# Mix stage of a two-block network: TensorE's order written out, with paired-half differential attention and retention interleaved with dense products

## Chip, cores and metric

One core of a Trainium2 chip (trn2) runs the whole network in one launch. The metric is the time of one execution on the device in microseconds (us). Of three runs shown the median was 3139.04 us, the lowest 3138.15 and the highest 3143.01.

## What is computed

All data are float32: 512 tokens (after the first block 528, with 16 learned tokens ahead of them) of 1024 features. A first block (attention of three kinds, then a wide feed-forward layer) is followed by two layers of a second block. Each of these two layers is a feed-forward layer, a *mix* stage and another feed-forward layer. The mix stage, with h the normalized input:

```
proj = h @ w_in                                   # 1024 -> 3584 columns
rq, rk, rv, rg, dq, dk, dv = split(proj)          # 512 columns each
# differential attention, 4 heads, each with two maps m of 64 features:
s[m] = q[m] @ k[m].T / 8        (causal);  p[m] = softmax(s[m])
o    = (p[0] - lam * p[1]) @ v;  o = rmsnorm(o) * subln_w * (1 - lambda_init)
# retention, 4 heads of 128 features (q, k rotated by position):
o    = ((q @ k.T / sqrt(128)) * decay(i - j)) @ v;  o = layernorm(o) * gn_w * silu(rg)
x    = x + concat(o_retention, o_diff) @ w_out
```

In the first layer all 528 rows are computed, in the second only the 512 that are returned (keys and values still have 528).

## The kernel before

Activations lie feature-major: 8 tiles of 128 features by 528 tokens. Every operand of a dense product is held as a high and a low part (`fp32r`), and a product is three passes: high by high, high by low, low by high. A *dense product* (`gemm`, line 163) makes one 128-row tile of the result: 8 slices of the 1024 features by 3 passes by 2 segments of 264 tokens, 48 matmuls into two PSUM tiles `ps_g` (line 172). Where 512 tokens are wanted it is 24 matmuls of 512 columns. Weights come in blocks of 256 columns (`wblock`, line 156): one 512 KB load each per 1024 elements on SP's queue, a copy to the high part on ScalarE (line 139) and a subtraction to the low part on VectorE (line 140).

`mix` (line 1217) runs through these steps: products for the values of differential attention (`v_heads`, `v_major`, transposed to token-major with the first 16 tokens in a fifth slot); twice: products for q and k of two heads, rotation (`rotate`, line 1378), split into halves (`stack`, line 1398), and `diff_heads` (line 1434) on the two heads; products for the values of retention; twice: products for q and k of two heads and `ret_head` (line 1510) for each; the norm of differential attention's output (lines 1272 to 1284); products for the gates with Silu (lines 1285 to 1292); the norm of retention's output (lines 1293 to 1306); the output products.

A block of differential attention (`diff_block`, line 1452) takes 128 queries (block 0: the 16 learned tokens; the second layer has no block 0) against all keys up to them: 16, 144, 272, 400 or 528 columns. For each of the two maps the scores are a 128-row matmul (line 1467: the stationary tile holds q's high half above its low half, the moving tile k's high half twice), a 64-row matmul with k's low half (line 1468) and the causal mask, added on the diagonal as a bf16 matmul with the identity (line 1470). The last block's 528 columns are cut into two spans of 264. Then come the maximum (1472), the exponential with its sum (1479), two reciprocals, a pass that scales the second map (1487), a pass that joins the maps (1490), transposes on TensorE (1497, and 1501 for the 16 first keys) with their copies (1498, 1502), and the product with V: 128-row matmuls for whole blocks of keys (1504) and one with 16 rows for the first keys (1505). Matmuls of float32 that is not split, such as 1504, 1505, 1525 and 1534, are two instructions each. `diff_heads` orders the three parts of consecutive blocks one behind the other.

Outside the mix stage the first block has an attention of blocks (line 546): four 64-row score matmuls a head, on rows 0 to 63 for one head of a pair and on rows 64 to 127 for the other (line 760).

What sets the order: the program gives instructions with their data; a scheduler lays them out per engine before the run, by priority and by when their operands should be there, so dense products may be put between the steps of attention wherever TensorE would wait. Each engine then runs its own list strictly in that order, and waits on semaphores.

## Time and profile before

| | |
|---|---|
| median of three runs | 3139.04 us |
| profiled execution | 3133.03 us, its span 3131.2 us |
| instructions | 54851 |
| TensorE matmuls busy | 3101.2 us |
| VectorE busy | 2250.4 us |
| ScalarE busy | 1534.7 us |
| mean granted TensorE clock | 0.996 |

The profiled execution is one of its own, near the runs shown. PE is TensorE's matmul side, PEld its weight loads, DVE VectorE, ACT ScalarE, POOL GpSimd, SP the engine whose queue issues most loads. A duration of a matmul runs from its start to a modelled end and overlaps its neighbours, so what TensorE pays for one is the distance to the next start. A form such as `64*128 64x264 f32` means 64 rows of the array, a stationary tile of 128 columns, 264 moving columns. Idle time before a group is given with what ended it.

### The profile page before, as it was taken

The page shows a single profiled execution, that of the slowest core. Times are in us where ns is not written, and L with a number is a line of the kernel's source. Part 1 is how long each engine was busy: PE and PEld are TensorE (multiplying, and loading weights), DVE is VectorE, ACT ScalarE, POOL GpSimd, SP SyncE. Part 2 cuts the span into 40 slices and gives each one's busy share as a digit, 9 for nine tenths or more (in the row PEclk, how much of TensorE's full clock was granted, in tenths as well). Part 3 has the DMA queues.
Part 4 walks back from the last instruction along what each step waited for, and adds up shares of the span by engine and source line. Part 5 has one row for each costly group of instructions (what it writes and reads, how often), then busy time and mean ns, then how long its engine had stood idle before and what let it go on. Part 6 is the DMA issues. An engine that isn't in the chain of part 4 may idle for free.

```text
span 3131.2 us, 54851 instructions
## 1 busy us (share of the span) xinstructions
PE 3101.2 (99%) x22264; PEld 2869.7 (92%) x22264; DVE 2250.4 (72%) x4225; ACT 1534.7 (49%) x2968; POOL 30.9 (1%) x64
## 2 busy tenths in 40 slices
PE   8999999999999999999999999999999999999998
PEld 6876798989898999999889999999999988899998
DVE  6256677977878887775866877768777586687775
ACT  5346556655555554444643544444444464354443
POOL 1000000000000000000000000000000000000000
PEclk9999999999999999999999999999999999999999
DMA  6121256323233422332112232322323311223232
GB/s 212 60 66 60 89 166 202 105 88 102 101 108 101 135 78 93 102 118 87 52 55 78 82 102 89 101 95 95 102 94 111 100 58 62 71 82 108 95 108 75
DMA packets 96958, 304.41 MB, mean 97 GB/s; under 512 B 12199, under 2 KB 20799, under 8 KB 96576
## 3 DMA queue, kind: packets, MB, share of 16 engines
q1 hardware_dynamic: 90384, 286.63, 27.8%
q0 software_dynamic: 2720, 7.78, 0.8%
q10 hardware_dynamic: 3600, 6.49, 0.7%
q8 instruction: 174, 2.85, 0.4%
q14 instruction: 80, 0.66, 0.1%
HBM read 290.34 MB, written 14.45 MB: 97 GB/s over the span
## 4 chain that ended last, share of the span: by engine, by line
PE 95%; DMA 2%; DVE 1%; ACT 1%; issue 0%; ACTq 0%; SPq 0%; DVEq 0%
PE ps_g L172 35%; PE ps_g L278 18%; PE ps_g L276 9%; PE ps_s L172 8%; PE ps_g L206 7%; PE ps_o L276 5%; PE ps_g L579 2%; PE ps_o L206 1%; DMA tmp_p<-gates 1%; PE ps_s L1468 1%; PE ps_s L513 1%; PE ps_o L535 1%; PE ps_s L1525 1%; PE ps_o L1504 1%; PE ps_o L1534 1%; PE ps_t L494 1%
## 5 line engine op out<-in xcount | busy, mean ns | idle before, releaser
L140 DVE TENSOR_TENSOR wqL<-wraw,wqH 128x512 fp32r<-128x512 f32 (+1 forms) x676 | 604.9, 910 | 278.2 <-ACT wqH L139 270.7
L139 ACT CAST wqH<-wraw 128x512 fp32r<-128x512 f32 (+1 forms) x676 | 527.1, 796 | 511.2 <-PE ps_g L172 282.5
L172 PE MATMUL ps_g<-yL,wqH 128*128 128x264 f32 (+2 forms) x1520 | 429.7, 320 | 0.4 <-DVE yL L414 0.4
L172 PE MATMUL ps_g<-yH,wqH 128*128 128x264 f32 (+2 forms) x1520 | 429.6, 321 | 0.0
L172 PE MATMUL ps_g<-yH,wqL 128*128 128x264 f32 (+2 forms) x1520 | 429.0, 321 | 0.3 <-DVE wqL L140 0.2
L278 PE MATMUL ps_g<-t,wqH 128*128 128x256 f32 (+1 forms) x1760 | 326.5, 283 | 0.0
L172 PEld LDWEIGHTS ps_g<-yL,wqH 128*128 128x128 f32 x1520 | 264.1, 189 | 23.7 <-issue 4.2
L172 PEld LDWEIGHTS ps_g<-yH,wqH 128*128 128x128 f32 x1520 | 262.6, 189 | 21.6 <-issue 3.1
L172 PEld LDWEIGHTS ps_g<-yH,wqL 128*128 128x128 f32 x1520 | 262.4, 189 | 21.0 <-issue 2.6
L278 PEld LDWEIGHTS ps_g<-t,wqH 128*128 128x128 f32 x1760 | 272.3, 188 | 1.8
L278 PE MATMUL ps_g<-t,wqL 128*128 128x256 f32 (+1 forms) x880 | 248.4, 282 | 0.0
L139 ACT CAST wqH<-ws 128x1024 fp32r<-128x1024 f32 x100 | 105.2, 1052 | 126.4 <-PE ps_o L276 33.6
L278 PEld LDWEIGHTS ps_g<-t,wqL 128*128 128x128 f32 x880 | 165.9, 189 | 0.0
L276 PE MATMUL ps_g<-t,wqH 128*128 128x264 f32 (+1 forms) x800 | 148.5, 283 | 0.0
L172 PE MATMUL ps_s<-hL,wqH 128*128 128x264 f32 (+1 forms) x544 | 141.2, 317 | 0.0
L172 PE MATMUL ps_g<-hL,wqH 128*128 128x264 f32 (+1 forms) x544 | 141.2, 317 | 0.0
L172 PE MATMUL ps_g<-hH,wqL 128*128 128x264 f32 (+1 forms) x544 | 141.1, 317 | 0.0
L172 PE MATMUL ps_s<-hH,wqL 128*128 128x264 f32 (+1 forms) x544 | 141.1, 317 | 0.0
L172 PE MATMUL ps_g<-hH,wqH 128*128 128x264 f32 (+1 forms) x544 | 141.0, 317 | 0.0
L172 PE MATMUL ps_s<-hH,wqH 128*128 128x264 f32 (+1 forms) x544 | 140.9, 316 | 0.0
L258 DVE TENSOR_TENSOR ws<-wraw 128x512 f32<-128x512 f32 x100 | 69.2, 692 | 86.1 <-DMA wraw<-in_ffn_w_gate 34.8
L140 DVE TENSOR_TENSOR wqL<-ws,wqH 128x1024 fp32r<-128x1024 f32 x100 | 122.4, 1224 | 6.3 <-ACT wqH L139 2.6
(445 smaller groups left out, 8234.8 us busy)
## 6 DMA issues: line engine op xcount, KB each, us to landing
wraw<-in_ffn_w_gate SPq DMA_DIRECT2D x88, 512.0 KB, 3.6
wraw<-in_ffn_w_up SPq DMA_DIRECT2D x88, 512.0 KB, 3.6
wraw<-in_ffn_w_down SPq DMA_DIRECT2D x88, 512.0 KB, 3.5
wraw<-in_w_in SPq DMA_DIRECT2D x86, 512.0 KB, 3.7
wraw<-in_w_up SPq DMA_DIRECT2D x64, 512.0 KB, 3.7
wraw<-in_w_down SPq DMA_DIRECT2D x32, 512.0 KB, 3.5
wraw<-in_w_gate SPq DMA_DIRECT2D x24, 512.0 KB, 4.1
tmp_p<-gates ACTq DMA_DIRECT2D x24, 256.0 KB, 3.3
```

What stands on the lines that cost most here:

```text
L139: self.nc.scalar.copy(out=H, in_=raw)
L140: self.nc.vector.tensor_sub(out=L, in0=raw, in1=H.bitcast(F32))
L172: self.nc.tensor.matmul(t[:, :m], lhsT=a, rhs=b[:, o:o + m], start=(k == 0 and i == 0), stop=(k == nk - 1 and i == 2))
L206: self.nc.tensor.matmul(q[:, :m], lhsT=a, rhs=b[:, o:o + m], start=(k == 0 and i == 0), stop=(k == nk - 1 and i == 2))
L258: nc.vector.tensor_add(out=S[:, :512], in0=A21, in1=A22)
L276: nc.tensor.matmul(ps, lhsT=a, rhs=b, start=first, stop=last)
L278: nc.tensor.matmul(ps, lhsT=a, rhs=b, start=False, stop=last, skip_group_check=True)
L494: nc.tensor.transpose(pt[:, s * P:(s + 1) * P], p[:, s * P:(s + 1) * P], self.ident)
L513: nc.tensor.matmul(ps[:, c], lhsT=q[:, i * P:(i + 1) * P], rhs=k[:, lo * P:(i + 1) * P], start=True, stop=True)
L535: nc.tensor.matmul(ops[obase:obase + 64, i * P:(i + 1) * P], lhsT=V(kb), rhs=pT[:, s0:s0 + P], start=(kb == lo), stop=(kb == i))
L579: nc.tensor.matmul(ps[:, :256], lhsT=a[:, ts], rhs=w, start=(k == 0 and i == 0), stop=(k == KD - 1 and i == 2))
L1468: nc.tensor.matmul(ps[:nq, :e - a], lhsT=qm[r], rhs=k[2][r, a:e], start=False, stop=not dg)
```

## The change

- Dense products become generators that yield after each of their eight slices; `drain` runs one to its end, `weave` runs a main generator and, between its steps, an even share of the steps of a side generator.
- In `mix` TensorE's instructions are kept in the order in which the program gives them (`manual_schedule`); other engines are laid out as before. The two pairs of heads of differential attention (three steps a block: scores; V product of the block before the last; transposes of the last) run against the products for retention's values and against the gates. Retention's first pair runs against q and k of its second pair, the second pair against the norm and the output products of differential attention, and the norm of retention's output against the rest of these.
- Scores: for each span and map three 64-row matmuls, high by high, low by high, high by low, the two maps alternating on rows 0 to 63 and 64 to 127; then the masks. The last block is cut into 512 columns (PSUM tiles `ps_s`) and the first 16 (PSUM tiles `ps_g`). `parts` replaces `stack`: q is scaled before the split, and q and k have one high and one low tile each.
- Softmax: the maxima come negated; the second map is scaled by lambda and the ratio of the sums in the pass that joins the maps; the output is scaled by the reciprocal when it leaves PSUM. The pass of line 1487 is gone.
- V product: the first 16 keys are transposed as 128 columns and multiplied as a 128-row matmul, with V's fifth slot filled with zeros by POOL (block 0 keeps 16 rows).
- Weight blocks are asked for one block ahead of use; the rotation tables have two buffers for three; retention's outputs share buffers with the values; differential attention's output goes into tiles of the stage's input; the loads of the last output weights are issued after the stage.

```diff
+def drain(steps):
+    while True:
+        try:
+            next(steps)
+        except StopIteration as e:
+            return e.value
+
+def weave(main, n, side, m):
+    done = 0
+    for i, _ in enumerate(main):
+        while done < (i + 1) * m // n:
+            next(side, None)
+            done += 1
...
-    def gemm(self, W, n, ys, R, seg_outer=False, tag="g"):
+    def gemm_steps(self, W, n, ys, R, seg_outer=False, tag="g"):
...
                         self.nc.tensor.matmul(t[:, :m], lhsT=a, rhs=b[:, o:o + m],
                                               start=(k == 0 and i == 0), stop=(k == nk - 1 and i == 2))
+                yield
         return ps
+    def gemm(self, *args, **kw):
+        return drain(self.gemm_steps(*args, **kw))
...
+            order = [2, 3, 6, 7, 4, 5, 12, 13, 8, 9, 10, 11]
+            def wi(i):
+                for j in order[:2] if i not in order else order[:order.index(i) + 2]:
+                    if j not in blocks:
+                        blocks[j] = self.wblock(A["w_in2"][l, j], KD, step=1024)
+                return blocks[i]
...
+            def gates():
+                for i in (12, 13):
+                    for n in range(2):
+                        g = self.tmp("sg", 4)
+                        self.evac_mul(g, (yield from self.gemm_steps(wi(i), n, ys, R)), rb)
+                        nc.scalar.activation(out=g[:, s], in_=g[:, s], func=AF.Silu)
+                        sg.append(g)
...
+            with self.tc.manual_schedule(engines={nc.tensor.engine}):
+                drain(values(0, NMETA, V))
+                rot = self.rot_tables("rope", rb)
+                drain(queries(2, "diff"))
+                side = values(6, 0, U)
+                weave(diff(0), 6 * nb, side, 32)
+                drain(side)
+                drain(queries(4, "diff"))
+                rot = self.rot_tables("ret", rb)
+                side = gates()
+                weave(diff(2), 6 * nb, side, 32)
+                drain(side)
+                drain(queries(8, "ret"))
+                main, side = retain(0), queries(10, "ret")
+                weave(main, 24, side, 32)
+                drain(side)
+                main, side = retain(2), chain(diff_out(), out_a())
+                weave(main, 24, side, 20)
+                weave(ret_out(), 4, side, 16)
+                drain(side)
+            W = self.last_w(A["w_out2b"][l])
...
-            t = self.qp.tile([P, TT], F32, name="rot", tag="rot", bufs=3)
+            t = self.qp.tile([P, TT], F32, name="rot", tag="rot", bufs=2)
...
-    def stack(self, t, R, key):
...
+    def parts(self, t, R, scale=None):
+        H, L = [self.tmp("qk2", 10, dt=F32R) for _ in range(2)]
+        self.split(t, H, L, R.off, R.n, scale)
+        return H, L
...
-        out = self.qp.tile([P, 5, P], F32, name="vh", tag="vh", bufs=6)
+        out = self.qp.tile([P, 5, P], F32, name="vh", tag="vh", bufs=8)
+        nc.gpsimd.memset(out[:, 4], 0.0)
...
                 step = self.diff_block(b, lam, *args)
                 next(step)
+                yield
+                if last:
+                    next(last, None)
+                yield
                 if todo:
                     next(todo)
-                if last:
-                    next(last, None)
+                yield
                 last, todo = todo, step
-        if last:
-            next(last, None)
+        next(last, None)
         next(todo)
         next(todo, None)
...
+        spans = [(0, nk)] if nk <= 512 else [(NMETA, nk), (0, NMETA)]
+        r = [slice(64 * m, 64 * m + 64) for m in range(2)]
+        qs = slice(q0, q0 + nq)
+        pst = []
+        for i, (a, e) in enumerate(spans):
+            ps = [self.psum("sg"[i])[:nq, :e - a] for _ in range(2)]
+            for j, (x, y) in enumerate(((0, 0), (1, 0), (0, 1))):
+                for m in range(2):
+                    nc.tensor.matmul(ps[m], lhsT=q[x][r[m], qs], rhs=k[y][r[m], a:e], start=(j == 0),
+                                     stop=(j == 2 and i == 1))
+            if i == 0:
+                for m in range(2):
+                    nc.tensor.matmul(ps[m][:, e - a - nq:], lhsT=self.identb[:nq, :nq], rhs=self.dm[:nq, :nq],
+                                     start=False, stop=True)
+            pst.append(ps)
...
+        nc.vector.reciprocal(out=sm[:nq, 8:10], in_=sm[:nq, 4:6])
+        nc.vector.scalar_tensor_tensor(out=sm[:nq, 10:11], in0=sm[:nq, 4:5], scalar=sm[:nq, 9:10], in1=lam[:nq],
+                                       op0=ALU.mult, op1=ALU.mult)
         a = Pm[0]
+        nc.vector.scalar_tensor_tensor(out=a[:nq, :nk], in0=Pm[1][:nq, :nk], scalar=sm[:nq, 10:11], in1=a[:nq, :nk],
+                                       op0=ALU.mult, op1=ALU.add)
         yield
...
         for j in range(b):
+            nc.tensor.matmul(ops[:nq, :P], lhsT=aT[:, j * P:(j + 1) * P], rhs=V[:, j], start=(j == 0), stop=False)
+        kk = 16 if b == 0 else P
+        nc.tensor.matmul(ops[:nq, :P], lhsT=aT[:kk, m], rhs=V[:kk, 4], start=(b == 0), stop=True)
+        nc.vector.tensor_scalar(out=o_sb[:nq, b], in0=ops[:nq, :P], scalar1=sm[:nq, 8:9], scalar2=None, op0=ALU.mult)
```

`ret_head` yields after each score span and each output block: 11 steps a head. `values` and `queries` make the products for V, or for q and k, of two blocks of weights; `diff_out`, `out_a` and `ret_out` hold the former lines 1272 to 1284, 1307 to 1310 and 1294 to 1306, the first and the last with a yield after each head.

## Rows read from the trace of the kernel before

**Rows 1.** The page, part 1: busy us and share of each engine

```profile
PE 3101.2 (99%) x22264; PEld 2869.7 (92%) x22264; DVE 2250.4 (72%) x4225; ACT 1534.7 (49%) x2968; POOL 30.9 (1%) x64
```

**Rows 2.** Busy time by windows, both mix stages (PEclk, DMA, GB/s last)

```profile
1440.00:1748.00 308.00, 306.77 (x2320) 280.27 (x2320) 203.99 (x555) 144.37 (x371) 0.00 (x0) 1.00 0.20 65
2472.00:2769.00 297.00, 296.90 (x1989) 259.34 (x1988) 195.58 (x495) 137.93 (x335) 0.00 (x0) 1.00 0.20 67
```

**Rows 3.** Waits of TensorE, first mix stage (total us, times, longest)

```profile
PE ps_s L1525 <- DVE rw L1526: 0.9, 1, 0.9
PE ps_s L1467 <- ACT tmp_P L1479: 0.3, 1, 0.3
```

**Rows 4.** Timeline of TensorE, 1512.9 to 1516.4 (start us, duration us)

```profile
1512.93 0.28 PE L1467 MATMUL ps_s<-tmp_qk,tmp_qk 128*128 128x264 f32 x1
1513.14 0.39 PE L1468 MATMUL ps_s<-tmp_qk,tmp_qk 64*128 64x264 f32 x1
1513.46 0.39 PE L172 MATMUL ps_g<-yH,wqL 128*128 128x264 f32 x1
1513.68 0.28 PE L172 MATMUL ps_g<-yH,wqH 128*128 128x264 f32 x1
...
1514.57 0.83 PE L1504 MATMUL ps_o<-vh,tmp_aT 128*128 128x128 f32 x6
1515.33 0.48 PE L1505 MATMUL ps_o<-vh,tmp_aT 16*128 16x128 f32 x2
1515.75 0.51 PE L172 MATMUL ps_g<-yL,wqH 128*128 128x264 f32 x2
1516.10 0.41 PE L172 MATMUL ps_g<-yH,wqL 128*128 128x264 f32 x2
1516.34 0.41 PE L172 MATMUL ps_g<-yH,wqH 128*128 128x264 f32 x2
```

**Rows 5.** Lines 1468 and 1505 in the whole kernel (duration ns min/median/max)

```profile
L1468 PE MATMUL ps_s<-tmp_qk,tmp_qk x88: 179/385/452, 1489.9 to 2612.4; 64*128 64x264 f32 x32, 64*128 64x144 f32 x16, 64*128 64x272 f32 x16, 64*128 64x400 f32 x16
...
L1505 PE MATMUL ps_o<-vh,tmp_aT x72: 267/274/372, 1503.9 to 2619.6; 16*128 16x128 f32 x64, 16*16 16x128 f32 x8
```

**Rows 6.** Busy time by windows, TensorE's instructions of line 546 alone

```profile
121.16:121.70 0.54, 0.54 (x4) 1.00 0.00 0
121.71:122.15 0.44, 0.44 (x10) 1.00 0.78 214
```

**Rows 7.** Groups of instructions, first mix stage: softmax (busy us, mean ns)

```profile
L1472 DVE TENSOR_REDUCE sm<-ps_s 128x1 f32<-128x400 f32 x8 | 4.6, 570 | 1.8 <-PE ps_s L1470 1.7
L1477 DVE TENSOR_SCALAR sm<-sm 128x1 f32<-128x1 f32 x32 | 4.5, 143 | 0.1
...
L1490 DVE SCALAR_TENSOR_TENSOR tmp_P<-tmp_P,sm 128x528 f32<-128x528 f32 x4 | 3.0, 757 | 0.0
...
L1479 ACT ACTIVATION_READ_ACCUMULATOR tmp_P<-ps_s,sm 128x1 f32 x40 | 7.7, 193 | 0.0
...
L1479 ACT ACTIVATE tmp_P<-ps_s,sm 128x400 f32<-128x400 f32 x8 | 4.7, 586 | 1.4 <-DVE sm L1485 1.4
...
L1479 ACT ACTIVATE tmp_P<-ps_s,sm 16x16 f32<-16x16 f32 x8 | 2.1, 264 | 1.4 <-DVE sm L1477 1.3
...
L1498 ACT COPY tmp_aT<-ps_t 128x512 f32<-128x512 f32 x4 | 2.3, 574 | 0.0
```

**Rows 8.** Timeline of ScalarE around the table load for Silu, layer 0

```profile
1678.59 0.27 ACT L1282 ACTIVATE tmp_qk<-ps_o,vecs 128x16 fp32r<-128x16 f32 x1 [0.32 <-PE ps_o L1335]
1678.88 1.28 ACT L1291 ACT_TABLE_LOAD   x1
1680.20 0.65 ACT L1291 ACTIVATE tmp_sg<-tmp_sg 128x528 f32<-128x528 f32 x1
```

**Rows 9.** Groups of instructions, first mix stage: retention's output on VectorE

```profile
L1299 DVE TENSOR_SCALAR ro<-ro,rst,sd 128x128 f32<-128x128 f32 x16 | 4.5, 332 | 0.0
...
L1538 DVE BATCH_NORM_STATS2 bst<-ro 16x6 f32<-16x128 f32 x4 | 1.1, 282 | 3.1 <-ACT ro L1536 3.1
```

More of the change, by code (lines that the diff above doesn't have):

```diff
@@ L2 @@
 from contextlib import ExitStack
+from itertools import chain
 import numpy as np
@@ L1228, in mix @@
             lam = self.lam(l)
[L1229 to L1240 removed]
+            order = [2, 3, 6, 7, 4, 5, 12, 13, 8, 9, 10, 11]
+            blocks = {i: w for i, w in enumerate(self.pre)}
+            def wi(i):
[3 more added lines that the diff above has]
+                return blocks[i]
+            V, U, sg = {}, {}, []
             od = [qp.tile([P, 5, P], F32, name="od", tag="od", bufs=4) for _ in range(4)]
@@ L1307, in mix, with values @@
-            for nb in range(4):
-                W = self.wblock(A["w_out2a"][l, nb], 4, step=1024)
-                for n in range(2):
-                    self.add_x(self.gemm(W, n, yd, R), 2 * nb + n)
+            nb = 5 if R.off == 0 else 4
+            def values(i0, c0, out):
+                late = None
+                for h in range(4):
+                    ps = yield from self.gemm_steps(wi(i0 + h // 2), h % 2, ys, R2, i0 == 0 and h == 0)
+                    if i0 == 0 and h == 0:
+                        self.late()
+                    if late:
+                        out[h - 1] = late()
+                    late = self.v_heads(ps, rb, c0)
+                self.vlate = lambda: out.update({3: late()})
@@ new lines, in queries @@
+            def queries(i0, use):
+                out = []
+                for j in range(2):
+                    for n in range(2):
+                        ps = yield from self.gemm_steps(wi(i0 + j), n, ys, (R, R2)[j] if use == "diff" else R2)
+                        if self.vlate:
+                            self.vlate()
+                            self.vlate = None
+                        if use == "diff":
+                            out.append(self.parts(self.rotate(ps, rot, True), (R, R2)[j], None if j else SCALE))
+                        else:
+                            out.append(self.rotate(ps, rot, False))
+                self.qk = out[:2], out[2:]
@@ new lines, in out_a, with ret_out @@
+            def out_a():
+                for b in range(4):
+                    W = self.wblock(A["w_out2a"][l, b], 4, step=1024)
+                    for n in range(2):
+                        self.add_x((yield from self.gemm_steps(W, n, yd, R)), 2 * b + n)
+            def ret_out():
+                rc = self.rsqrt_small(rst[:, :, :, 1], 1.0, 1.0)
+                for h in range(4):
+                    o, p = ro[h], sg[h]
+                    for b in range(5):
+                        nq = P if b < 4 else NMETA
+                        nc.vector.tensor_scalar(out=o[:nq, b], in0=o[:nq, b], scalar1=rst[:nq, h, b, 0:1],
+                                                scalar2=rc[:nq, h, b:b + 1], op0=ALU.subtract, op1=ALU.mult)
+                    for pt, c0, m in self.feature_major(o, 0, R):
+                        sl = slice(c0, c0 + m)
+                        nc.vector.scalar_tensor_tensor(out=p[:, sl], in0=pt, scalar=self.v(f"gn_w_{l}", h), in1=p[:, sl],
+                                                       op0=ALU.mult, op1=ALU.mult)
+                    yr.append(self.y_tile(4 + h))
+                    self.split(p, yr[h][0], yr[h][1], R.off, R.n)
+                    yield
@@ L1364, in lam @@
         nc.scalar.activation(out=e[:, :2], in_=ps[:, :2], func=AF.Exp)
-        nc.vector.scalar_tensor_tensor(out=e[:, 2:3], in0=e[:, 0:1], scalar=li, in1=e[:, 1:2], op0=ALU.add, op1=ALU.subtract)
+        nc.vector.scalar_tensor_tensor(out=e[:, 2:3], in0=e[:, 1:2], scalar=-li, in1=e[:, 0:1], op0=ALU.add, op1=ALU.subtract)
         return e[:, 2:3]
@@ L1460, in diff_block @@
+        for i, ps in enumerate(pst):
+            for m in range(2):
+                c = 2 * i + m
+                nc.vector.tensor_reduce(out=sm[:nq, c:c + 1], in_=ps[m], axis=AX.X, op=ALU.max, negate=True)
+        if len(spans) == 2:
+            nc.vector.tensor_tensor(out=sm[:nq, 0:2], in0=sm[:nq, 0:2], in1=sm[:nq, 2:4], op=ALU.min)
+        Pm = [self.tmp("P", 4) for _ in range(2)]
         for m in range(2):
-            qm, km, r = q[m][:, q0:q0 + nq], k[m], slice(64 * m, 64 * m + 64)
@@ L1481, in diff_block @@
[L1481 to L1488 removed]
+                c = 4 + 2 * i + m
```

171 lines of the change are left out of this document (47 added, 124 removed).

## Prediction

> **What bounds the kernel now.** I read the page first: TensorE is busy for 99% of the span, so a microsecond less on its queue is a microsecond of the kernel wherever it stays fed [rows 1]. Then the busy time of the two mix stages, the only stretches that the change touches: 308 and 297 us, TensorE full in both at a granted clock of 1.00, VectorE at two thirds, ScalarE under half, DMA at 0.20 [rows 2]. Then TensorE's waits in the first of them: 1.2 us in all; in the second the view lists none [rows 3]. So the order that was found for TensorE keeps it fed, and time can be won only by work that it need not do, and lost by new waits. Last the timeline, to see what its work costs, since durations overlap and only the distance from one start to the next counts.
>
> **What a change of the row group costs.** In [rows 4] two dense 264-column matmuls start 0.24 us apart, 0.12 each. Around a 64-row score matmul (line 1468, 1513.14) the distances are 0.21 for the 128-row one before it, 0.32 for itself and 0.22 for the dense one after it: 0.75 where three take 0.36. One excursion out of the 128-row form and back costs 0.39 us beyond its columns. The 16-row pair of line 1505 shows the same: six matmuls before it take 0.76 (0.11 each and 0.10 more), the pair 0.42 (0.20 more), and the two dense ones after it 0.35 (0.11 more).
>
> **What the change removes.** Today every 64-row matmul stands alone between 128-row ones: 88 excursions in the two layers. The 16-row products are two instructions each, so the 64 with 128 query columns are 32 excursions [rows 5].
> - Scores: six 64-row matmuls now stand together per span and block. The first layer has five blocks per head with one span each and a second span in the last: 6 excursions a head; the second has 5. For four heads that is 24 + 20 = 44, so 44 fewer.
> - The product with V takes the first 16 keys as a full 128-row matmul against zeroed rows, so 32 excursions go; the columns stay.
> - 76 x 0.39 = 29.6 us. Block 0 of the first layer (four heads) has one change more between 64 and 16 rows, about 0.8 back.
> - Columns: four score passes per key column become six, three deep if the halves run side by side. Line 546 in the first block works on rows 0 to 63 for one head and on rows 64 to 127 for the next: the stretch where one follows the other holds 10 such matmuls in 0.44 us, the stretch before it 4 in 0.54 [rows 6]. So halves do overlap. The saved pass is 1344 columns a head, 1344/264 x 0.12 = 0.6 us, 4.9 us for eight heads at most; narrow spans still have their weights to load, so the lower end is 0. I take 1, as two of the five spans are narrow.
>
> Gain on TensorE: 30 us (29 to 34).
>
> Off TensorE the change drops one VectorE pass over the probabilities and three small operations per block, and some half-height copies of q and k. I cost that at nothing: VectorE has a third of the stage free. The POOL fills, the sign of lambda, the smaller rotation buffer (its second pair is loaded a whole interleaved step before use), values and retention outputs in one buffer, and weight blocks asked for one block earlier on SP's queue also cost nothing: DMA is at 0.20, and no wait of TensorE in [rows 3] ends on a weight. If that cover were gone, a late block would show as a wait on the split weights.
>
> **What the fixed order adds.** Where TensorE waits now, everything behind it waits, dense products too. A step of eight-part dense work is six matmuls, 0.72 us.
> - *End of each attention weave (four).* Transposes of the last block come after four dense steps (2.9), the V product of block 2 (six at 0.11), four transposes (0.45) and the V product of block 3 (0.88): 4.9 us after its scores. Its softmax: two maxima of 512 columns (0.57 x 512/400 = 0.73 each), two narrow ones and their minimum as small operations of 0.15 (0.45), exponentials 2 x (0.75 + 0.19) + 2 x (0.26 + 0.19) = 2.8, three small operations (0.45), the last pass 0.76: 5.9, less 0.6 that the first span runs ahead, 5.3 [rows 7]. With up to two passes of 0.6 ahead of it on a queue it is late by 0.4 to 1.6; I take 1.2. Then the V product waits for a copy of 0.57, less a transpose, some 0.8 with the signal. 2 each, 8 in all (4 to 16).
> - *Silu between exponentials.* The gate products fill the second weave of each layer. Each Silu (0.65) then has a table load of 1.28 ahead of it and one behind it for the next exponential [rows 8]: 3.2 us on ScalarE, four times a layer. In the middle of a weave the slot of the last block is some 6.3 us against a chain of 5.3, of block 3 about 7 against 3.7, so part is absorbed: late by 0 to 2.2. I take 0.5, 4 in all (0 to 18).
> - *Start of each attention weave (four).* The first scores need the rotated, split k of head 0, which has one product (48 matmuls, 5.8 us) to be ready; two copies, the rotation's passes and a split are some nine operations between 0.4 and the 0.76 of the widest pass [rows 7], so 3.6 to 6.8. Late by 0 to 1.0: I take 0.5, 2 in all.
> - *Retention's output.* Its transposes follow the last retention step with one dense step between. Copy, two steps of statistics, square root, reciprocal (0.15 to 0.3 each, as the first of them) and the first of five scalings of 0.33 [rows 9] make some 1.6, then transposes at the pace of the scalings instead of 0.11, and VectorE loaded through four heads: 2.5 a layer, 5 in all (3 to 10). Today dense gate products lie here.
> - *Start of the mix.* Two small matmuls of the norm now stand back to back with a square root and a reciprocal between them, small operations again: 0 to 1 each, 1 in all.
>
> New waits 20, less the 1.2 that stand there now: 19 (7 to 45). **Sum: -30 + 19, -11 to -12 us.** The profiled execution took 3133.03 (span 3131.2), 6.0 under the median of 3139.04; against the median I forecast 3127.
>
> **A rule against the change.** The row shows the load 0.02 us behind the operation ahead of it, and the Silu 0.04 behind the load, so a switch costs ScalarE 1.3 [rows 8]. The Trainium skill ("ScalarE: Activation LUTs", section What ACT_TABLE_LOAD costs) gives 1283 ns for the load and another 1380 ns of drain for every switch to a different set. The trace agrees on the load and shows no drain here. By the page's figures, were they to reach TensorE whole, 16 switches more would add 22 us to the sum, 3149 (an estimate from that page).
>
> **Rivals.**
> 1. *Softmax later than its slot in every block (slower).* The place is the transpose of each of the 36 blocks; each microsecond of mean lateness costs 36 us. My sum holds 12 of it (0.33 each). At a mean of 1.0 the kernel gets 24 more: 3151. It decides, slower by 0.2%, from 0.85. For it: in-order queues on VectorE and ScalarE with bursts, and a slot that is only 1 us longer than the longest chain. Against: VectorE's shorter chain and a third of its time free.
> 2. *All chains in time.* The waits shrink to about 6: -24, 3115. For it: today's order waits 1.2. Against: the end of a weave is short by arithmetic.
> 3. *Halves one after the other.* Three more passes of 1344 columns for eight heads, 1344/264 x 0.12 x 24 = 14.7: 3142. [Rows 6] speak against it.
> 4. *The six matmuls do not stay together*, so that the score excursions remain: the gain is 32 x 0.39 = 12.5, against 19 of waits, +6: 3145. The written order speaks against it.
> 5. *Dearer table switches.* If a drain of about the load's own length came with each of the 16 loads and reached TensorE whole, some 16 x 1.3 = 21 more: 3148. [Rows 8] show none. (This is what the page named above would make of it.)
>
> **How the numbers follow.** About 0.2%, 6.3 us, is what a measurement can tell. Forecast 0.42 (its own range 3119 to 3135, nearly all of it faster), rival 1 0.22, rival 2 0.16, rival 3 0.08, rival 4 0.05, rival 5 0.04, the rest 0.03 on either side. Faster: nine tenths of 0.42 and 0.16, 0.54. Within 0.2%: a tenth of the forecast, most of rivals 3 and part of 1 and 4, 0.17. Slower 0.29. Since both signs are likely the range reaches from the far side of rival 2 with full columns, 3109, to rival 1, 3151.
>
> **What would show it.** Right: 64-row matmuls in pairs that start a few nanoseconds apart; no 16-row matmul but in block 0; TensorE's own work in the two stages some 30 us less; waits of 10 to 25 us, most on the transposes that end a weave and on retention's output. Wrong: waits on the transposes of every block; 64-row matmuls spaced by their own length; idle time in the gate weave ending on an exponential behind a table load; a dense product waiting for weights.

## The result, and the profile after

The changed kernel takes 3165.97 us (median of four runs, 3157.87 to 3167.78), the kernel before 3138.6 beside it on the same chip: a ratio of 1.008, interval 1.006 to 1.010. It is slower by 0.8%; 3127 was forecast, in a range up to 3151. The profiled execution took 3167.78, its span is 3166.0.

First the page of the changed kernel, part 1, for [rows 1]. VectorE has 25 us less to do, as the dropped passes said, and TensorE is still busy for 98%:

```profile
PE 3096.6 (98%) x22352; PEld 2871.5 (91%) x22352; DVE 2225.6 (70%) x4085; ACT 1522.5 (48%) x2922; POOL 33.4 (1%) x80
```

The two mix stages of the changed kernel by windows, for [rows 2]. In each stretch the distance from its length to the first busy number is TensorE's idle time, 15.8 and 20.6 us where there were 1.2 and 0.1; and PEclk, the granted clock, is 0.97 and 0.96 where it was 1.00:

```profile
1446.42:1764.54 318.12, 302.33 (x2367) 279.81 (x2366) 192.33 (x480) 137.81 (x348) 1.23 (x8) 0.97 0.19 63
2488.31:2804.51 316.20, 295.56 (x2027) 260.51 (x2026) 185.61 (x432) 132.71 (x311) 1.23 (x8) 0.96 0.19 63
```

TensorE's waits in the first and the second mix stage, for [rows 3]. Where two lines stood there are twenty-one:

```profile
PE ps_o L1575 <- ACT tmp_aT L1570: 3.9, 4, 1.8
PE ps_o L1577 <- ACT tmp_aT L1573: 2.8, 4, 0.9
PE ps_s L1597 <- DVE rw L1598: 2.1, 1, 2.1
PE ps_o L1575 <- ACT tmp_aT L1564: 1.6, 2, 0.8
PE ps_s L1397 <- DVE ro L1348: 1.1, 1, 1.1
...
PE ps_t L1560 <- DVE tmp_P L1553: 0.4, 2, 0.2
```

```profile
PE ps_s L1528 <- ACT tmp_P L1545: 4.8, 6, 1.3
PE ps_o L1575 <- ACT tmp_aT L1570: 4.3, 4, 1.8
PE ps_t L1560 <- DVE tmp_P L1553: 3.5, 3, 1.9
PE ps_s L1597 <- DVE rw L1598: 2.3, 1, 2.3
PE ps_o L1575 <- ACT vh L1490: 2.1, 2, 1.1
PE ps_s L1397 <- DVE ro L1348: 1.1, 1, 1.1
...
```

The softmax's operations in the first stage, by groups, for [rows 7]. They are about as long as forecast (0.73, 0.75 and 0.76), so the length of its passes was not what was misjudged:

```profile
L1538 DVE TENSOR_REDUCE sm<-ps_s 128x1 f32<-128x512 f32 x8 | 5.1, 684 | 0.2
...
L1545 ACT ACTIVATE tmp_P<-ps_s,sm 128x512 f32<-128x512 f32 x8 | 5.5, 683 | 4.7 <-DVE sm L1540 4.7
...
L1553 DVE SCALAR_TENSOR_TENSOR tmp_P<-tmp_P,sm 128x528 f32<-128x528 f32 x4 | 3.1, 768 | 0.1
```

The lower clock comes in eight stretches of the two stages, 41.0 us in all, and each begins inside a wait of TensorE or at most 1.2 us behind its end. This is TensorE's timeline of the changed kernel around the longest one in the first layer:

```profile
1686.53 1.05 PE L1597 MATMUL ps_s<-tmp_qk,tmp_qk 128*128 128x264 f32 x4
1687.66 0.66 PE L1397 MATMUL ps_s<-ident,od 128*128 128x128 f32 x4
1688.25 0.23 PE L1402 MATMUL ps_o<-ident,od 16*128 16x16 f32 x1
1690.57 0.94 PE L1597 MATMUL ps_s<-tmp_qk,tmp_qk 128*128 128x400 f32 x2 [2.09 <-DVE rw L1598]
1691.85 1.11 PE L1397 MATMUL ps_s<-ident,od 128*128 128x128 f32 x4 [0.34 <-DVE yL L1332]
...
1698.46 0.81 PE L192 MATMUL ps_g<-yH,wqH 128*128 128x264 f32 x2
1699.06 0.64 PE L192 MATMUL ps_g<-yL,wqH 128*128 128x264 f32 x2
1699.50 0.64 PE L192 MATMUL ps_g<-yH,wqL 128*128 128x264 f32 x2
```

And the stretch itself by windows:

```profile
1691.75:1701.99 10.24, 9.60 (x37) 7.32 (x38) 4.69 (x15) 3.09 (x8) 0.00 (x0) 0.50 0.09 29
```

Here retention's scores alternate with the transposes of differential attention's norm, and no dense product lies between. The score tile waits 2.09 us for VectorE; then the granted clock is 0.50, the lower level (1.2 GHz). VectorE's timeline shows what stands ahead of the pass to `rw` that frees the tile: a weight split (line 159) and two passes of the last rotation of retention's second pair (lines 1461 and 1462):

```profile
1687.17 0.43 DVE L1598 TENSOR_TENSOR rw<-ps_s,tmp_D 128x264 f32<-128x264 f32 x1 [2.40 <-PE ps_s L1597]
1687.56 1.23 DVE L159 TENSOR_TENSOR wqL<-wraw,wqH 128x1024 fp32r<-128x1024 f32 x1
1688.70 0.85 DVE L1461 TENSOR_TENSOR tmp_qk<-ps_g,rot 128x264 f32<-128x264 f32 x2
1689.47 0.70 DVE L1462 TENSOR_TENSOR tmp_t<-tmp_t,rot 128x528 f32<-128x528 f32 x1
1690.09 0.42 DVE L1598 TENSOR_TENSOR rw<-ps_s,tmp_D 128x264 f32<-128x264 f32 x1
```

Two dense pairs inside the stretch start 0.44 us apart (1699.06, 1699.50); at the full clock they start 0.24 apart [rows 4]. So nearly half of the busy time in such a stretch is lost. It ends after dense products have come back at 1698.46.

This gives an accounting. The span of a stage is TensorE's idle time, plus half of its busy time where the granted clock is 0.5, plus the rest, its own work at the full clock. (Half is an estimate that holds up: e10_free_plain below, with 136.5 us at the lower clock, comes out at the own work of e1_free, 579.2 and 580.2.) For both stages together:

| us | before | after | forecast of the difference | found |
|---|---|---|---|---|
| own work | 603.2 | 578.6 | -30 | -24.6 |
| idle | 1.3 | 36.4 | +19 | +35.1 |
| lost to the lower clock | 0 | 19.3 | none | +19.3 |
| both stages | 604.6 | 634.3 | -11 | +29.8 |

The medians differ by 27.4. (The profiled spans differ by 34.8; nearly all of the rest lies in the first 65 us, which the change does not touch.)

### The profile page after: what moved, and what is told of

Its sections match the earlier page's. It is cut to its first block, busy times and chain, and to the rows that moved or that the text cites. A ratio compares the mean times of both kernels' runs of the same rounds, so it can differ in the third digit from the quotient of the medians.

```text
span 3166.0 us, 54847 instructions
## 1 busy us (share of the span) xinstructions
PE 3096.6 (98%) x22352; PEld 2871.5 (91%) x22352; DVE 2225.6 (70%) x4085; ACT 1522.5 (48%) x2922; POOL 33.4 (1%) x80
## 4 chain that ended last, share of the span: by engine, by line
PE 93%; DVE 3%; ACT 3%; DMA 2%; issue 1%; DVEq 0%; SPq 0%; ACTq 0%
PE ps_g L192 34%; PE ps_g L302 18%; PE ps_g L300 9%; PE ps_s L192 8%; PE ps_g L230 7%; PE ps_o L300 5%; PE ps_g L603 1%; PE ps_o L230 1%; PE ps_s L537 1%; PE ps_o L559 1%; ACT tmp_P L1545 1%; PE ps_s L1597 1%; PE ps_o L1607 1%; PE ps_o L1575 1%; DMA num<-in_x 1%
## 5 line engine op out<-in xcount | busy, mean ns | idle before, releaser
L192 PE MATMUL ps_g<-yH,wqH 128*128 128x264 f32 (+2 forms) x1616 | 470.2, 332 | 0.0
L192 PE MATMUL ps_g<-yL,wqH 128*128 128x264 f32 (+2 forms) x1616 | 449.8, 319 | 0.1
L192 PE MATMUL ps_g<-yH,wqL 128*128 128x264 f32 (+2 forms) x1616 | 449.4, 319 | 0.0
L192 PEld LDWEIGHTS ps_g<-yH,wqH 128*128 128x128 f32 x1616 | 280.7, 191 | 25.5 <-issue 5.7
L192 PEld LDWEIGHTS ps_g<-yL,wqH 128*128 128x128 f32 x1616 | 281.1, 191 | 21.7 <-issue 4.0
L192 PEld LDWEIGHTS ps_g<-yH,wqL 128*128 128x128 f32 x1616 | 279.5, 190 | 20.4 <-issue 2.2
```

The costliest lines, as they stand in the source:

```text
L192: self.nc.tensor.matmul(t[:, :m], lhsT=a, rhs=b[:, o:o + m], start=(k == 0 and i == 0), stop=(k == nk - 1 and i == 2))
```

## Experiments

In free order the same arithmetic is faster than both kernels. The table has the accounting of every run, both stages together, taken from its one profiled execution, and the ratio of its time to that of the kernel before; the sections below refer to it.

| kernel | idle | at clock 0.5 | lost to it | own work | both stages | median | ratio, interval |
|---|---|---|---|---|---|---|---|
| before | 1.3 | 0 | 0 | 603.2 | 604.6 | 3138.6 | |
| after | 36.4 | 41.0 | 19.3 | 578.6 | 634.3 | 3166.0 | 1.008 (1.006, 1.010) |
| e1_free | 4.8 | 0 | 0 | 580.2 | 585.0 | 3119.4 | 0.9932 (0.9915, 0.9948) |
| e2_old_attn | 33.6 | 71.7 | 34.2 | 603.7 | 671.6 | 3198.1 | 1.0185 (1.0158, 1.0213) |
| e3_silu_late | 35.7 | 30.7 | 14.6 | 580.0 | 630.3 | 3163.9 | 1.0079 (1.0064, 1.0094) |
| e4_fill | 34.5 | 20.5 | 9.7 | 585.7 | 629.9 | 3163.2 | 1.008 (1.0065, 1.0095) |
| e5_early_t | 27.1 | 34.1 | 16.0 | 577.8 | 620.9 | 3155.1 | 1.004 (1.0028, 1.0053) |
| e6_tail | 34.2 | 20.5 | 9.9 | 579.5 | 623.5 | 3157.3 | 1.0056 (1.0043, 1.007) |
| e7_mended | 25.2 | 13.7 | 6.8 | 578.3 | 610.3 | 3142.0 | 1.0005 (0.9995, 1.0015) |
| e8_free_serial | 3.8 | 3.4 | 1.7 | 580.6 | 586.1 | 3118.9 | 0.993 (0.9918, 0.9943) |
| e9_free_old_v | 4.5 | 0 | 0 | 590.1 | 594.6 | 3128.1 | 0.9969 (0.9957, 0.9981) |
| e10_free_plain | 34.9 | 136.5 | 60.4 | 579.2 | 674.5 | 3205.2 | 1.0202 (1.0182, 1.0222) |
| e11_end_only | 10.7 | 17.1 | 8.2 | 580.6 | 599.4 | 3133.3 | 0.998 (0.9972, 0.9989) |
| e12_plain_own | 20.4 | 34.1 | 12.6 | 590.5 | 623.5 | 3155.9 | 1.0052 (1.0037, 1.0067) |
| e13_silu_after | 32.7 | 23.9 | 11.1 | 578.8 | 622.6 | 3153.9 | 1.0057 (1.0043, 1.0072) |
| e14_mended_silu | 22.0 | 10.2 | 4.7 | 577.5 | 604.2 | 3140.3 | 0.9999 (0.9989, 1.0009) |

The sum of the two stages follows the medians to about 4 us (e1_free: -19.5 in the stages, -19 in the time; e10_free_plain: +69.9 and +67) in all but e2_old_attn (+67.0 and +59.5; its four runs lie 19 us apart), so little else is at work.

**The order or the arithmetic.** e1_free leaves TensorE's order to the scheduler, with all else as changed:

```diff
-            with self.tc.manual_schedule(engines={nc.tensor.engine}):
+            if True:
```

> The changed kernel, but TensorE's order is left to the scheduler again; the paired attention, the V product with 128 rows and the order in the program stay. Theory (waits of the written order and the half-rate clock behind them outweigh a real saving of work): in the two mix stages idle time of TensorE falls from 36 us to under 8, no stretch at clock 0.5 is left, its own work stays some 25 us under the kernel before, and the time is 3110 to 3122. Rival (the new form of attention costs the time, not the order): still 3150 or more.

It took 3119.4. The two mix stages of e1_free by windows: TensorE nearly full again, the granted clock 1.00:

```profile
1449.10:1747.41 298.31, 295.59 (x2367) 275.69 (x2366) 190.98 (x480) 137.80 (x348) 1.23 (x8) 1.00 0.21 67
2471.21:2757.94 286.73, 284.65 (x2028) 252.98 (x2026) 183.59 (x432) 132.70 (x311) 1.23 (x8) 1.00 0.21 69
```

So the whole loss is the fixed order, 46.6 us between two kernels that differ in it alone. The rest of the change, the arithmetic together with the interleaving in the program and the buffers, gains 19; TensorE's own work falls by 23.0.

e2_old_attn is the other half of the cross: the written order, with scores and V product as before (128 + 64 rows, with `stack` for `parts`; 16 rows). The last block stays cut into 512 and 16 columns.

```diff
-            for j, (x, y) in enumerate(((0, 0), (1, 0), (0, 1))):
-                for m in range(2):
-                    nc.tensor.matmul(ps[m], lhsT=q[x][r[m], qs], rhs=k[y][r[m], a:e], start=(j == 0),
-                                     stop=(j == 2 and i == 1))
+            for m in range(2):
+                nc.tensor.matmul(ps[m], lhsT=q[m][:, qs], rhs=k[m][:, a:e], start=True, stop=False)
+                nc.tensor.matmul(ps[m], lhsT=q[m][r[m], qs], rhs=k[2][r[m], a:e], start=False, stop=(i == 1))
...
-        kk = 16 if b == 0 else P
+        kk = 16
```

> The changed kernel with the written order, but scores as before (a 128-row matmul and one with 64 rows per map and span) and 16 rows for the first keys in the V product. Theory (the paired form saves 25 us of TensorE's work in the two stages, as 76 excursions at 0.39 less what it adds): 3166 plus 18 to 30, so 3184 to 3196. Rival (the paired form saves nothing, halves do not run side by side): 3160 to 3172.

Own work rose by 25.1, back to that of before; idle time stayed. But the lower clock grew from 41 to 72 us, so the run fell 32 behind the changed kernel. The fourth cell of the cross, the old attention in free order in the interleaved program, was not run.

**V's share, and whether halves must alternate.** e9_free_old_v is e1_free with 16 rows in V:

```diff
-        kk = 16 if b == 0 else P
+        kk = 16
```

> Edit: free order, and the product with V takes the first 16 keys as a 16-row matmul again (the scores stay in halves). Theory (every change of row group costs 0.39 us, and 32 excursions of V are 12.5 us of the saving): own work of the stages rises from 580.2 to 590 to 594, the time from 3119.4 to 3128 to 3134. Rival (nearly all of the saving is that of the scores): own work under 585, the time under 3125.

Own work 590.1, time 3128.1: V is worth 9.9 us of TensorE's work for 32 excursions, 0.31 each; the scores have the other 13.1 of the 23.0. e8_free_serial is e1_free with the three matmuls of one map given before those of the other:

```diff
-            for j, (x, y) in enumerate(((0, 0), (1, 0), (0, 1))):
-                for m in range(2):
+            for m in range(2):
+                for j, (x, y) in enumerate(((0, 0), (1, 0), (0, 1))):
```

> Edit: the changed kernel without the written order (as the run with the order left to the scheduler, 3119.4), and the six 64-row score matmuls of a span given map after map instead of alternating between rows 0 to 63 and 64 to 127. Theory (halves overlap in pairs that start a few nanoseconds apart; three passes' columns saved, 14.7 us by the columns of the whole kernel): the matmuls of one map run one after another, own work of the stages rises by 10 to 16 us over the 580.2 of the run in free order, and the time is 3129 to 3136. Rival (the halves overlap whenever the queue holds matmuls of both, since the second map's three can start beside the first map's last, or the row group's change is what counts): own work within 4 us, 3117 to 3124.

The rival was right: own work 580.6, time 3118.9. Six matmuls of 400 columns, first alternating (timeline of e1_free), then map after map (e8_free_serial):

```profile
1533.31 0.81 PE L1528 MATMUL ps_s<-tmp_qk,tmp_qk 64*128 64x400 f32 x6
```

```profile
1530.67 0.82 PE L1528 MATMUL ps_s<-tmp_qk,tmp_qk 64*128 64x400 f32 x6
```

Three passes of 400 columns take 0.55 at the dense pace (264 in 0.12), six would take 1.1 (an estimate from [rows 4]). So the halves overlap in both runs. Which order reached TensorE in the second is not shown: in free order the scheduler may have alternated the maps again, and the rows do not tell one map from the other.

**What the program's order is worth to the scheduler.** e10_free_plain leaves out the interleaving in the program as well, in free order: all five `weave` calls get no side steps.

```diff
-                weave(diff(0), 6 * nb, side, 32)
+                weave(diff(0), 6 * nb, side, 0)
...
-                weave(ret_out(), 4, side, 16)
+                weave(ret_out(), 4, side, 0)
```

> Edit: free order, and no interleaving in the program either: each main generator runs to its end before its side products are given, so the arithmetic alone is left of the change. Theory (the scheduler puts the dense products into the gaps by itself, the written interleaving gives nothing): idle of the stages 3 to 8, the time 3116 to 3124. Rival (the scheduler keeps near the order of the program, and the interleaving is what keeps TensorE fed): idle 15 or more, 3130 or more.

3205.2, the slowest of all. 18 us near the start of the first attention by windows, dense matmuls (line 192) alone, in e10_free_plain and then in e12_plain_own (below):

```profile
1501.40:1519.40 18.00, 0.00 (x0) 0.00 (x0) 0.50 0.09 28
```

```profile
1501.40:1519.40 18.00, 8.96 (x56) 7.02 (x54) 1.00 0.09 30
```

No dense matmul at all, and the clock is at its lower level. e12_plain_own changes the PSUM tiles of the 16-column scores alone:

```diff
-            ps = [self.psum("sg"[i])[:nq, :e - a] for _ in range(2)]
+            ps = [self.psum(("ss", "to")[i][m])[:nq, :e - a] for m in range(2)]
```

> Edit: as the run without any interleaving (3205.2), but the scores of the first 16 columns go into the one ps_t and the one ps_o tile instead of two of the four ps_g tiles that dense products need. Theory (a tile's buffers are handed out in the order of the program, so dense products that are given after attention cannot start before its ps_g tiles are read, and TensorE has nothing to fill with): dense matmuls lie between the steps of the first heads, idle of the stages falls from 34.9 to 4 to 14, loss at clock 0.5 from 60 to under 20, the time 3118 to 3145. Rival (the scheduler keeps near the order of the program whatever the tiles): idle 25 or more, loss 40 or more, 3180 or more.

It is 49 us faster than e10_free_plain, and dense matmuls are back: the changed kernel's use of `ps_g` for scores had shut them out, because later products could not have those buffers sooner. Idle is 20.4, not 4 to 14, and the time is above the 3118 to 3145 of the theory: most of what is left lies in the unwoven end of the stage (the norms), and own work is 10 more than in e1_free; these runs do not show why. The interleaving does help, as the order in which a scheduler is given the work: with the tiles of the changed kernel it is worth 86 us (e10_free_plain against e1_free). e1_free is faster than e12_plain_own too, by 36, but these two differ in the tiles as well.

**Which waits.** Four edits of the written order. e5_early_t transposes and copies the first keys' probabilities one step earlier:

```diff
+        if b == 4:
+            pt = self.psum("g")
+            nc.tensor.transpose(pt[:, :P], a[:, :P], self.ident)
+            nc.scalar.copy(out=aT[:, m], in_=pt[:, :P])
...
         yield
         ops = self.psum("o")
...
-            nc.tensor.transpose(ops[:, P:2 * P], a[:, :P], self.ident)
-            nc.scalar.copy(out=aT[:, m], in_=ops[:, P:2 * P])
```

> Edit: in the order as written, the transpose of the first 16 keys' probabilities and its copy move from the step of the V product into the step of the transposes before it, so a dense step lies between the copy and the V product. Theory (the waits of the V product on that copy, 3.9 + 2.8 in the first layer and 4.3 in the second, are waits for work given too late, and each is followed by the risk of a stretch at clock 0.5): the waits on lines 1570 and 1573 are gone, idle time of the two stages falls from 36.4 to 25 to 28 us, the time lost at clock 0.5 does not rise above 19, and the run takes 3148 to 3158. Rival (the softmax itself is late, and the wait only shows where the order first meets it): the same idle time appears at the transposes, 33 us or more in all, and the run stays at 3162 to 3170.

Idle fell by 9.3, the time by 10.8. The waits on lines 1570 and 1573 are gone (2.6 of their 11.0 us come back as waits on the copy of line 1564), so these were waits for work given too late.

e6_tail puts dense steps of the next products ahead of the last transposes and the last V product of a weave:

```diff
-                side = values(6, 0, U)
-                weave(diff(0), 6 * nb, side, 32)
+                side = chain(values(6, 0, U), queries(4, "diff"))
+                weave(diff(0), 6 * nb + 4, side, 38)
...
+        yield
+        yield
         next(todo)
```

> Edit: in the order as written, the last transposes and the last V product of a pair of heads get two steps more of dense work ahead of each, taken from the products that follow. Theory (8 us of the waits are the ends of the four weaves, where the softmax is longer than its slot): idle of the stages falls from 36.4 to 29 to 32, the time lost at clock 0.5 by 0 to 5, the run takes 3153 to 3162. Rival (spreading the same dense steps more thinly makes every other slot shorter, so the waits move to the middle of the weaves): idle 35 or more, the run 3162 or more.

The time, 3157.3, is as the theory had it, but by another way: idle fell by 2.2 only (29 to 32 was expected, 34.2 found), the loss to the clock by 9.4.

e7_mended joins both and makes the last rotation ready sooner:

```diff
-                weave(main, 24, side, 32)
+                weave(main, 22, side, 40)
```

> Edit: both of the two edits just described, and a weave of retention's first pair that gives its side products 40 steps to 22 instead of 32 to 24, so that the last rotation is ready sooner. Theory (waits are what loses the gain, and the low clock follows waits): idle of the stages 15 to 24 against 36.4, loss at clock 0.5 from 5 to 15 against 19.3, the run 3133 to 3150. Rival (a written order keeps some 35 us of waits wherever the steps lie): 3160 or more. A third view, that the low clock has nothing to do with the waits: idle falls to 15 to 24 but the loss stays at 19 or more, 3147 to 3157.

Idle -11.2 (to 25.2, just above the 15 to 24 of the theory), clock -12.5, time 3142.0. With the rotation earlier, the score tile's waits of 2.1 and 2.3 on `rw` are gone. Waits and the loss to the clock fell together in these three runs, but in no fixed proportion: by 9.3 and 3.3 (e5_early_t), 2.2 and 9.4 (e6_tail), 11.2 and 12.5 here.

e4_fill adds six unread dense matmuls behind each head of differential attention's norm:

```diff
+            def fill(n=6):
+                ps, y = self.psum("g"), ys[KD - 1][0]
+                for i in range(n):
+                    nc.tensor.matmul(ps[:, :264], lhsT=y[:, :P], rhs=y[:, :264], start=True, stop=True)
...
+                    fill()
```

> The changed kernel with six dense matmuls (264 columns, a result that nobody reads) behind each of the four steps of the differential norm in the retention weave: 0.73 us a step, 5.8 us of added work in two layers. Theory (TensorE waits there and lacks dense work, and that is what halves the clock for the 10.2 us behind it): both stretches of 10.2 us at 0.5 vanish, idle time falls by 3 us or more, and the kernel is faster by 3 to 9 us in spite of the added work: 3157 to 3163. Rival (the half-rate clock has nothing to do with what TensorE does there): it keeps its stretches and gets slower by 2 to 6 us.

The 10.24 us stretches there are down to 3.41 in the first layer and gone in the second, and 7.1 us of added work costs the whole kernel nothing that can be measured. The added work takes the place of part of the waits for `rw`, which are 1.2 and 1.5 instead of 2.1 and 2.3, but idle time fell by 1.9 and not by 3, and the time, 3163.2, is at the upper end of the theory's 3157 to 3163. A new stretch of 6.83 at the lower clock came at 2622.83, in a weave that the edit does not touch.

**Silu.** e3_silu_late moved the four Silu passes in the program behind the second weave:

> The changed kernel with the four Silu passes of a layer moved behind the weave, so that no table is switched between exponentials. If the table loads delay the softmax: idle time of the two second weaves falls from 9.5 us to under 4 and the 3.4 us at clock 0.5 at their ends go, 3154 to 3161. Rival (the waits come from the place of a block's own steps; the first weaves, without a Silu, wait 9.0 us as well): 3162 to 3168.

```diff
-                        nc.scalar.activation(out=g[:, s], in_=g[:, s], func=AF.Silu)
...
+                for g in sg:
+                    nc.scalar.activation(out=g[:, s], in_=g[:, s], func=AF.Silu)
```

It told nothing of Silu, since only TensorE's order is fixed by the program. (The waits of the second weaves in the changed kernel add up to 13.9 us and those of the first to 12.4, not to the 9.5 and 9.0 of the expectation.) The timeline of ScalarE in e3_silu_late shows the loads where they were:

```profile
1599.80 1.28 ACT L1370 ACT_TABLE_LOAD   x1
1601.09 0.65 ACT L1370 ACTIVATE tmp_sg<-tmp_sg 128x528 f32<-128x528 f32 x1
```

The run shows something else. TensorE's instructions are those of the changed kernel in the same order, and idle time is nearly the same (35.7 against 36.4), yet the loss to the clock is 14.6 against 19.3. Nearly all of the difference lies in the end of the second layer's stage, from retention's first scores on, first in the changed kernel and then in e3_silu_late:

```profile
2693.27:2804.51 111.24, 106.89 (x693) 92.04 (x692) 72.32 (x181) 37.70 (x86) 0.00 (x0) 0.94 0.18 56
```

```profile
2694.59:2802.51 107.92, 103.38 (x694) 88.98 (x692) 72.18 (x181) 37.77 (x86) 0.00 (x0) 0.98 0.18 57
```

The longest waits there are 2.25 and 2.26 us, at the same matmul; behind it the clock is low for 10.24 us in one and for 3.41 in the other. So the loss of one trace can differ by 5 us with the waits unchanged, and a difference of that size in the table is not to be put down to an edit.

At the place of the loads above the changed kernel shows what such a load does. TensorE waits from 1601.5 to 1603.3 for the last line, a copy of 0.26:

```profile
1600.39 0.56 ACT L1564 COPY tmp_aT<-ps_t 128x512 f32<-128x512 f32 x1
1600.97 1.28 ACT L1545 ACT_TABLE_LOAD   x1
1602.26 0.38 ACT L1545 ACTIVATE tmp_P<-ps_s,sm 128x144 f32<-128x144 f32 x1
...
1602.99 0.26 ACT L1570 COPY tmp_aT<-ps_o 128x128 f32<-128x128 f32 x1
```

e13_silu_after makes Silu wait by its data, with a bias of zero from the last block of attention:

```diff
-                        nc.scalar.activation(out=g[:, s], in_=g[:, s], func=AF.Silu)
...
+                nc.vector.tensor_scalar(out=zero, in0=od[3][:, 4, 0:1], scalar1=0.0, scalar2=None, op0=ALU.mult)
+                for g in sg:
+                    nc.scalar.activation(out=g[:, s], in_=g[:, s], func=AF.Silu, bias=zero)
```

> Edit: Silu of the gates takes a bias of zero that is made from the last block of differential attention, so it cannot run before the second weave ends; the run that only moved it in the program still had its four table loads inside the weave. Theory (a table load and a Silu ahead of the exponentials make ScalarE's copies late, as at 1601.5, where the copy of the first keys stands behind a load and two exponentials): idle of the two stages falls from 36.4 to 28 to 33, the wait of 1.8 on line 1570 in the first layer is gone, loss at clock 0.5 does not rise above 19, the time 3150 to 3161. Rival (ScalarE has time enough, the waits come from the order on TensorE): idle 34.5 or more, 3161 to 3168.

Idle -3.7, clock -8.2, time 3153.9, 12 less than the changed kernel; the wait of 1.8 is gone. The waits that fell lie in the second weaves (5.2 to 3.6 and 9.0 to 6.8), where the gates are; of the fall of the clock's loss 5.0 lies there too, and the other 3.2 where the waits are nearly the same in both runs. So Silu's switches cost 3.7 us of waiting and about 5 of clock in their own place; that all of the 12 is theirs is not shown.

e14_mended_silu is e7_mended with the same edit of Silu.

> Edit: the three edits of the mended order and the late Silu together. Theory (every wait taken away gives its own length back and some of the low clock): idle from 25.2 to 16 to 22, loss at clock 0.5 of 0 to 7, the time 3127 to 3139. Rival (what is left of the waits are others, of score tiles and of the norms, and Silu falls on the retention's output instead): idle 23 or more, 3139 to 3150.

Idle 22.0, loss 4.7, 3140.3: idle and clock at or within the theory's bounds, the time 1.3 above its range and in that of the rival. Beside e7_mended the edit of Silu brought 1.7 us in the median, which the scatter of the runs covers. The mended order is level with the kernel before and still 21 us behind e1_free. What waits is left there are those on score tiles (4.0 in the second layer) and on copies and norms.

**Is the lower clock local.** e11_end_only fixes the order from retention's second pair to the end, and leaves the rest of the stage free:

```diff
-            with self.tc.manual_schedule(engines={nc.tensor.engine}):
+            if True:
...
+            with self.tc.manual_schedule(engines={nc.tensor.engine}):
                 main, side = retain(2), chain(diff_out(), out_a())
```

> Edit: written order only from the second pair of retention's heads to the end of the stage, free order before it. Theory (waits and the low clock are local: the low clock comes behind the waits of this part, whatever the part before it did): idle of about 8 in this part (3.9 in the first layer, 4.3 in the second), the two 10.2 us stretches at clock 0.5 there remain, loss 8 to 13, the time 3133 to 3142. Rival (the low clock needs the waits of the whole stage): the idle time remains but loss is under 4, 3124 to 3131.

3133.3. In the first layer the wait of 2.1 is followed by a stretch of 13.65 us at clock 0.50, though the stage ran nearly full until then:

```profile
1679.17:1692.82 13.65, 12.89 (x48) 9.80 (x48) 6.50 (x18) 3.08 (x8) 0.00 (x0) 0.50 0.16 53
```

In the second layer the same wait, 2.3, is followed by none. So the lower clock is local, but not every wait brings it; what decides between such cases these runs don't settle.

## Why the prediction was wrong, point by point

- **The step that failed most: the sum had no term for the clock.** It priced every wait at its own length and carried the granted clock of 1.00 over from [rows 2]. The runs showed 41 us at clock 0.5 in the changed kernel, 19.3 us lost, as much as all the waits that were forecast. Of the 40.8 us between the forecast of -11 and the +29.8 of the two stages, the clock has 19.3, the waits 16.1 and the gain 5.4. Without the clock the kernel would have taken about 3147, inside the range, but it would still have been slower than the kernel before: 35.1 us of new waits against 24.6 of saved work had turned the sign by themselves.
- **The waits were undersized: 36.4 against 20.** Of the named ones the ends of the weaves came to 1.7 + 1.8 + 1.7 + 2.7 = 8.0 (forecast 8, but 2.4 of it is the V product of block 3, which the forecast did not have), Silu to 3.7 (4), retention's output to 2.2 (5), the start of the mix to 1.2 (1), the starts of weaves to 0 (2). What was missing were waits in the middle: the first keys are transposed in the V product's own step, and its copy stands in ScalarE's queue behind the next block's exponentials (lines 1570 and 1573, 11.0 in all, of which 3.2 at the ends); scores that wait for their two `ps_s` tiles (line 1528, 5.6); 5.7 on `rw`, where VectorE has other work ahead and the norm of differential attention and retention have no dense product between them; and 2.7 behind the copy of the values (line 1490). The forecast looked for lateness in the softmax's own chain and not in the queue of copies behind it. The size was within its own bounds, though: it gave 7 to 45 (its items add up to 7 to 50), and 45 with a gain of 29 makes 3155, but the range stopped at rival 1, 3151.
- **The gain was oversized: 24.6 against 30.** The price of an excursion, 0.39, came from two places of one timeline [rows 4]; over 76 excursions it is 24.6/76 = 0.32, by e1_free, which needs no term for the clock, 23.0/76 = 0.30, and 0.31 for V alone (e9_free_old_v). The count held. This is line 1577 of the changed kernel, for [rows 5], with 16 rows in block 0 only:

```profile
L1577 PE MATMUL ps_o<-vh,tmp_aT x72: 264/275/421, 1506.3 to 2668.8; 128*128 128x128 f32 x64, 16*16 16x128 f32 x8
```

- *Rival 1* had the sign and not the place: transposes wait for the softmax's last pass (line 1560) for 3.9 us in all, a tenth of a microsecond a block, not 1.0. *Rival 2* is what happens in free order. *Rivals 3 and 4* fall: halves overlap (at 1529.2 of the changed kernel the 64-row matmuls start in pairs 4 to 6 ns apart), and the changed kernel's work fell.
- *Rival 5* falls in its form. The timeline of ScalarE above shows the load 0.02 behind the copy and the exponential 0.01 behind the load. The Trainium skill ("ScalarE: Activation LUTs", section What ACT_TABLE_LOAD costs) has another 1380 ns of drain; this trace shows the load of 1283 ns alone, as [rows 8] did. What the switches cost, some 9 us by e13_silu_after, came by TensorE's waits and its clock. The count was off as well: the changed kernel has 43 loads where there were 33, ten more and not 16.

## To carry to other kernels

Where a scheduler already keeps an engine fed, give it the interleaved order and the cheaper arithmetic, and don't fix the order: here that was worth 46.6 us, the difference between 0.8% slower and 0.7% faster. When a change brings waits to a TensorE that had none, add a term for the granted clock, as a range: in the changed kernel 36.4 us of waits came with 19.3 lost to it, and the same order of instructions lost 14.6 in another run. Before sharing PSUM buffers between two kinds of work, ask which of them must then wait for the other; and look in the trace whether an edit moved what it was to move.

## What was not expected of the hardware

- Waits of 1 to 2.3 us inside an otherwise full stage were followed by 3.4 to 13.7 us at half the clock; three close waits of 1.3, 0.8 and 1.5 at 2619 to 2625 in the changed kernel by none, while at the same place of e4_fill waits of 1.3, 0.8 and 1.0 went with 6.8 us of it. So a wait alone does not decide it, and what does these runs do not settle.
- 64-row matmuls of the two halves took no longer when the program gave three of one half before three of the other (e8_free_serial: 0.82 for 0.81), in free order, where the scheduler may have put them in pairs again.
- Long runs of short attention matmuls without dense products kept the clock low with few waits: in e10_free_plain by windows, 25.3 of 27.3 us busy, behind a wait of 2.4:

```profile
1501.03:1528.34 27.31, 25.34 (x113) 19.63 (x115) 13.95 (x47) 10.72 (x47) 0.00 (x0) 0.50 0.06 20
```
